# A two-block transformer step on one core: the chunked state-space part in another order

## The chip, the cores and the metric

The program runs as one launch on one core of a Trainium2 chip, in fp32 (matmuls on fp32 values split into two reduced parts). The metric is device time in microseconds, from the profiled execution and from timed runs. The engines: TensorE (PE in the rows; its weight loads PEld), VectorE (DVE), ScalarE (ACT), GpSimd (POOL), SyncE (SP), which issues most DMAs from one in-order queue.

## The reference, cut to what matters

272 tokens (16 meta tokens and 256 of x), width 1024. The first block has an attention half and a state-space half side by side, then a feed-forward part that picks single-neuron experts (PEER); the second block (two layers) follows and is not touched.

```
proj = rms_norm(h) @ w_in                       # q 512, k 128, v 128, u 512 columns
attn = sliding_window_attention(q, k, v)        # 8 heads, 2 key heads, sinks, 16 meta keys
# state-space half: 32 groups of 16 channels, each drives one 64-dim complex diagonal state
abar = exp((a_re + i a_im) * dt);  bbar = (abar - 1) / a * b
s_t  = abar * s_{t-1} + bbar @ u_t              # an associative scan over the 272 tokens
y    = Re(c @ s) + d * u
z    = gelu(y);  ssm = z * sigmoid(z @ glu_w + glu_b)
h    = h + concat(rms_norm(attn), rms_norm(ssm)) @ w_out
h    = h + peer_ffn(rms_norm(h))                # 8 heads x 16 experts of 16384
```

## The kernel before, in words

The state-space half is computed in 34 chunks of 8 tokens. `coefficients` makes the powers of abar (A), the discretized b (`bb`) and the maps `W` (8 taps by 16 channels into the 64 complex states of a group). `maps` transposes `W` on TensorE into `WT` and builds the rotation table `R` over the chunks. `enter` writes the projected rows u to DRAM and reads them back as `U`, chunk by chunk (the U bounce). `run` then multiplies U by WT (`st`, one input a chunk), rotates it by R, scans over the chunks (`sc`), rotates back (`S`), and forms y on TensorE from `T` (the response inside a chunk, a Toeplitz matrix) and from `G` (the outputs of the state). `outputs` builds `G` from c and A; `response` multiplies G by bd (bb spread out) into `K`, writes it to DRAM and reads it back 16 times shifted as `T`. After the Gelu, z goes to DRAM and comes back in another order as `zT`; the GLU matmuls follow, then the second half of the out-projection.

The big products lie in four scratch buffers t0 to t3 (`temp`), each handed from one tile to the next: a tile gets its buffer when all users of the tile before are done. PSUM banks are handed round in the same way, by tags: "p", "o", "y", "m" (transposes, scores, response) and "b" (state inputs, part of y, GLU).

`first_half` traces, in this order: the angles, the norm and its transposes (`turn`, whose `hH` ScalarE and `hL` VectorE write; the last `hL` is `c.split`), the u projection (four weight units of 128x1024, two of its eight row blocks each) with `coefficients` behind the first unit, then `enter`, `maps`, a 8 MB clearing of `wscr`, and then two strands that `Flow` interleaves: the state-space `run` in front, and as background `kv`, `q` and `attention` (with the first half of the out-projection, `out_part`). The numbers that both yield say how much of the background is traced between two steps of the front.

That tracing order is not the order of execution. A planner orders the instructions of each engine ahead of time: by its own cost model, it puts next what is ready, the one traced earliest first; something traced late that is ready early can go far ahead. `c.after(b, a)` (an order-only edge) keeps b behind a. The order of each engine and of SP's queue is then fixed in the program, and on the chip semaphores do the waiting.

Weights come through `Feed`: units of 512 KB are loaded by SP into five buffers, ScalarE rounds each to `H`, and GpSimd (P) or VectorE (V) subtracts to get `Lo`; `jobs` says which one per weight. Units 0 to 3 are wu, 4 and 5 wkv, 6 to 9 wq, 10 to 17 wo (10 to 13 for attention's half, 14 to 17 for the other), from 18 on wqy, the queries of PEER. A matmul of such values is three: H with H, and H with each Lo (lines 1678 to 1680).

Of the kernel before, what the change touches and what calls it, by code (L numbers as in the profile page):

```python
# [19 lines left out]
FT = mybir.dt.float32  # L20
# [4 lines left out]
OP = mybir.AluOpType  # L25
AX = mybir.AxisListType

T = 256
# [36 lines left out]
class Feed:  # L65


    def __init__(self, nc, wpool, spool, jobs, bufs, ahead):
        self.nc, self.wpool, self.spool, self.bufs, self.ahead = nc, wpool, spool, bufs, ahead
        self.units = []  # L70
        for ap, n, eng in jobs:
            for i in range(ap.shape[1]):
                self.units += [(ap[:, i, q * n:(q + 1) * n], n, eng[(2 * i + q) % len(eng)]) for q in range(2)]
        self.loaded = []
        self.cut = []
        self.taken = 0
        self.more = None
# [6 lines left out]
    def load(self, upto):  # L84
        while len(self.loaded) <= min(upto, len(self.units) - 1):
            ap, n, _ = self.units[len(self.loaded)]
            t = self.wpool.tile([128, 1024], FT, tag="w", name="w")[:, :n]
            self.nc.sync.dma_start(t, ap)
            self.loaded.append(t)
# [83 lines left out]
SJ = 8  # L173
# [3 lines left out]
def first_half(c):  # L177

    nc, tc, A = c.nc, c.tc, c.A
    V, G = nc.vector, nc.gpsimd  # L180
    f = Flow(c)
    with ExitStack() as ctx:
# [56 lines left out]
        for q in range(4):  # L239
            H, Lo = c.feed.take()  # L240
            for k2 in range(2):
                k = 2 * q + k2
                for ct in range(4):
                    s = slice(k2 * 512 + ct * 128, k2 * 512 + (ct + 1) * 128)
                    c.mm3(up[ct][:, :L], H[:, s], Lo[:, s], hH[:, k], hL[:, k], k == 0, k == 7)
                if k + 3 < 8:
                    turn(k + 3)
            if q == 0:
                ssm.coefficients()
        ssm.enter(up)  # L250
        ssm.maps()
        for i in range(4):
# [182 lines left out]
class Ssm:  # L435
# [9 lines left out]

    def product(self, re, im, a, b, t):

        V = self.V
        V.tensor_tensor(re, a[0], b[0], op=OP.mult)
        V.tensor_tensor(t[0], a[1], b[1], op=OP.mult)  # L450
        V.tensor_tensor(im, a[0], b[1], op=OP.mult)
        V.tensor_tensor(t[1], a[1], b[0], op=OP.mult)
        V.tensor_tensor(re, re, t[0], op=OP.subtract)
        V.tensor_tensor(im, im, t[1], op=OP.add)

# [27 lines left out]
    def coefficients(self):  # L483
# [28 lines left out]
        V.tensor_tensor(ci, t0, t1, op=OP.subtract)  # L512
        V.tensor_tensor(ci, ci, den, op=OP.mult)
        bre, bim = (P1(n).rearrange("p (j q) -> p j q", j=16) for n in ("bre", "bim"))
        bb = [one.tile([128, 16, 16], FT, name="bb%d" % i) for i in range(2)]
        shape = [128, 16, 16]
        cb = [t[:, :, None].to_broadcast(shape) for t in (cr, ci)]
        t = self.temp("tb", 2).rearrange("p (a j q) -> p a j q", j=16, q=16)
        self.product(bb[0], bb[1], (bre, bim), cb, [t[:, z] for z in range(2)])

        self.bd = [one.tile([128, 16, 2, 16], FT, name="bd%d" % i) for i in range(2)]
        for z in range(2):
            nc.gpsimd.memset(self.bd[z], 0.0)
            for g in range(2):
# [6 lines left out]
        t = [self.temp("tw", 2 + z) for z in range(2)]  # L531
        self.product(cut(self.W[0]), cut(self.W[1]), [A[:, z, :, :SJ, None].to_broadcast(shape) for z in range(2)],
                     [bb[z][:, :, None, :].to_broadcast(shape) for z in range(2)], [cut(x) for x in t])

    def enter(self, up):

        nc, c, one = self.nc, self.c, self.one
        uP = one.tile([128, 4 * L], FT, tag="uP", name="uP").rearrange("p (a j c) -> p a j c", a=4, j=SJ)
        self.U = U = one.tile([128, 32, SC], FT, name="U")
        for ct in range(4):  # L540
            nc.scalar.copy(uP[:, ct].rearrange("p j c -> p c j"), up[ct][:, :L].rearrange("p (c j) -> p c j", j=SJ))
            nc.sync.dma_start(c.udr[ct * 128:(ct + 1) * 128], uP[:, ct])
        src = c.udr.rearrange("(g q) j c -> q j g c", q=16)
        for j in range(SJ):
            m = SJ - 1 - j
            nc.sync.dma_start(U[16 * m:16 * m + 16], src[:, j])

    def maps(self):

        nc, c, V, P1, one = self.nc, self.c, self.V, self.P1, self.one  # L550
        self.WT = [one.tile([128, 16, 128], FT, tag="WT", name="WT", bufs=2) for z in range(2)]
        for z in range(2):
            for i in range(4):
                p = c.psum("m")
                for k in range(4):
                    nc.tensor.transpose(p[:, k * 128:(k + 1) * 128], self.W[z][:, (4 * i + k) * 128:(4 * i + k + 1) * 128], c.ident)
                nc.scalar.copy(self.WT[z][:, 4 * i:4 * i + 4].rearrange("p a b -> p (a b)"), p)

        self.R = R = one.tile([128, 2, 16, SC], FT, name="R")
        V.memset(R[:, 0, :, 0:1], 1.0)  # L560
        V.memset(R[:, 1, :, 0:1], 0.0)
        t = self.temp("tr", 2)[:, :512].rearrange("p (z j c) -> p z j c", z=2, j=16)
        for i in range(6):
            n = 2 ** i
            k = min(n, SC - n)
            self.product(R[:, 0, :, n:n + k], R[:, 1, :, n:n + k], [R[:, z, :, :k] for z in range(2)],
                         [self.cs[z][:, 1 + i, :, None].to_broadcast([128, 16, k]) for z in range(2)], [t[:, z, :, :k] for z in range(2)])
        self.mags = one.tile([128, 16, SC], FT, name="mags")
        nc.scalar.copy(self.mags, self.mag[:, 1, :, None].to_broadcast([128, 16, SC]))
        V.memset(self.mags[:, :, 0:1], 0.0)  # L570

    def outputs(self):

        nc, c, V, P1, one = self.nc, self.c, self.V, self.P1, self.one
        A = self.A
# [3 lines left out]
        a = [A[:, z, :, :, None].to_broadcast(shape) for z in range(2)]  # L579
        t = [self.temp("tg", 2 + z).rearrange("p (j m q) -> p j m q", j=16, q=16) for z in range(2)]  # L580
        V.tensor_tensor(self.G[0], C[0], a[0], op=OP.mult)
        V.tensor_tensor(t[0], C[1], a[1], op=OP.mult)
        V.tensor_tensor(self.G[0], self.G[0], t[0], op=OP.subtract)
        V.tensor_tensor(self.G[1], C[0], a[1], op=OP.mult)
        V.tensor_tensor(t[1], C[1], a[0], op=OP.mult)
        V.scalar_tensor_tensor(self.G[1], self.G[1], -1.0, t[1], op0=OP.mult, op1=OP.subtract)

    def response(self):
# [18 lines left out]
        nc.sync.dma_start(c.kdr.rearrange("(a p) n -> p a n", p=128), K.rearrange("p a m q -> p a (m q)"))  # L607
        self.T = [one.tile([128, 16, 128], FT, tag="WT", name="T", bufs=2) for z in range(2)]
        src = c.kdr.rearrange("(g q) n -> q g n", q=16)
        for h in range(2):  # L610
            for j in range(SJ):
                m = SJ - 1 - j
                nc.sync.dma_start(self.T[h][16 * m:16 * m + 16], src[:, 16 * h:16 * h + 16, 16 * m:16 * m + 128])

    def run(self, glu, out):
        nc, c, V, one = self.nc, self.c, self.V, self.one
        yield 8000

        st = self.temp("s", 0)[:, :2 * 16 * SC].rearrange("p (z j c) -> p z j c", z=2, j=16)
        for j0, n in ((0, 6), (6, 5), (11, 5)):  # L620
            for z in range(2):
# [5 lines left out]
                for g in range(2):  # L627
                    r = slice(64 * g, 64 * g + 64)
                    nc.scalar.copy(st[r, z, j0:j0 + n], v[r, :, g])
            yield 1500  # L630

        self.outputs()
        flat = lambda t: t.rearrange("p j c -> p (j c)")
# [6 lines left out]
        V.tensor_tensor(m1[:, 1], m1[:, 1], m2[:, 0], op=OP.subtract)  # L640
        yield 3000
        sc = room("sc", 3)
        for z in range(2):
            V.tensor_tensor_scan(flat(sc[:, z]), flat(self.mags), flat(m1[:, z]), 0.0, op0=OP.mult, op1=OP.add)
        yield 2000
        self.response()
        m1, m2 = room("m1", 0), room("m2", 1)
# [10 lines left out]
        yield 3000  # L658

# [4 lines left out]
        for ct in range(4):  # L664
            y = c.psum("yb"[ct % 2])
            for jj in range(4):
                j = 4 * ct + jj
                for g in range(2):
                    o = 2 * jj + g
                    m = nc.tensor.matmul(y[:, o * n:(o + 1) * n], self.T[j // 8][:, (2 * j + g) % 16], self.U[:, 2 * j + g, 2:],  # L670
                                         start=(o == 0), stop=False, skip_group_check=True)
# [9 lines left out]
            if ct % 2:  # L681
# [3 lines left out]
                for k in (ct - 1, ct):  # L685
                    nc.sync.dma_start(self.zT[:, k], c.zdr[k * 128:(k + 1) * 128].rearrange("p i c -> p (i c)"))
            yield 1500
        yield "exps"
        acc = [c.psum("b") for _ in range(2)]
        yield 8000  # L690
        for k in range(4):
            for co in range(4):
# [925 lines left out]
def body(tc, A, out):  # L1618
# [3 lines left out]
    with ExitStack() as ctx:  # L1622
# [23 lines left out]
        def evac(dst, src):  # L1646
# [3 lines left out]
            else:  # L1650
# [5 lines left out]
        LE = [P, P, V]  # L1656
        jobs = [(A["wu"], 1024, [P, P, V]), (A["wkv"], 1024, [P]), (A["wq"], 1024, [P]), (A["wo"][:, :2], 1024, [P, P, V]),
                (A["wo"][:, 2:], 1024, [P]), (A["wqy"], 1024, [P, V]),
                (A["ut"], 1024, [V]), (A["pv"], 1024, [V]), (A["we"], 1024, LE), (A["woe"], 1024, LE), (A["wod"][:, :2], 1024, LE),
# [213 lines left out]
```

## Time and profile before

| | before |
|---|---|
| median of 3 runs | 1415.31 us (1413.77 to 1418.36) |
| profiled execution | 1414.31 us, span 1412.3 us |
| TensorE busy | 1293.4 us (92%), mean granted clock 0.943 |
| VectorE busy | 935.5 us (66%) |
| ScalarE busy | 647.7 us (46%) |
| GpSimd busy | 457.5 us (32%) |
| HBM read, written | 233.24 MB, 28.90 MB |

Times inside the program are microseconds from the start of the span. "Busy" is the sum of the instructions' durations; neighbours on one engine overlap a little, so starts tell the pace better than durations. The granted clock of TensorE is a share of its full rate: 1.0 is 2.4 GHz, 0.5 is 1.2 GHz.

### The profile page before, as it was taken

The numbers are of one execution on the slowest core, as the hardware profiler recorded it, in microseconds if no ns is written. First come the engines' busy times: TensorE is split into PE (matmuls) and PEld (weight loads), VectorE is DVE, ScalarE is ACT, GpSimd is POOL, SyncE is SP. The second block draws the span as 40 slices with busy tenths as digits, with TensorE's granted clock in tenths as the row PEclk, the third lists the DMA queues.
The fourth block names the chain that finished last, engine by engine and source line by source line (L and its number), as shares of the span: only waits on it lengthen the run. The fifth ranks groups of instructions, "written<-read, shape, count | busy, mean of one in ns | idle before, by whom it ended". The sixth has DMA issues, their size and how long they took to land.

```text
span 1412.3 us, 21249 instructions
## 1 busy us (share of the span) xinstructions
PE 1293.4 (92%) x7800; PEld 1123.5 (80%) x7800; DVE 935.5 (66%) x2151; ACT 647.7 (46%) x1119; POOL 457.5 (32%) x237
## 2 busy tenths in 40 slices
PE   4566979899999999999899999999998989989998
PEld 3554868899999999999777888888876768765777
DVE  8845216889889766665578965555567775585834
ACT  4233315455455444444454444444454545433553
POOL 3140204257777878720000000000024226441243
PEclk9775769999999999999999999999999999997999
DMA  5653436478888777799799966566574335541331
GB/s 195 212 175 81 39 89 213 145 215 223 227 225 223 203 204 194 208 321 321 249 304 311 336 217 191 186 191 190 187 235 149 90 105 156 202 147 53 95 105 60
DMA packets 118520, 263.80 MB, mean 187 GB/s; under 512 B 36096, under 2 KB 50304, under 8 KB 117136
## 3 DMA queue, kind: packets, MB, share of 16 engines
q1 hardware_dynamic: 80336, 228.82, 51.6%
q0 software_dynamic: 20608, 8.46, 5.0%
q10 hardware_dynamic: 17472, 25.17, 5.0%
q8 instruction: 61, 1.00, 0.3%
q14 instruction: 43, 0.35, 0.1%
HBM read 233.24 MB, written 28.90 MB: 186 GB/s over the span
## 4 chain that ended last, share of the span: by engine, by line
PE 76%; DVE 16%; DMA 4%; issue 2%; ACT 2%; SPq 0%; DVEq 0%; ACTq 0%
PE ps L865 21%; PE ps L1678 9%; PE ps L1679 9%; PE ps L1680 9%; PE pr L1678 4%; PE pr L1680 4%; PE pr L1679 4%; DMA ga<-ascr 3%; PE m L1270 2%; PE ps L1078 2%; DVE Lo L102 2%; PE o L1315 1%; DVE rs L1695 1%; DVE rs L1696 1%; PE p L1678 1%
## 5 line engine op out<-in xcount | busy, mean ns | idle before, releaser
L101 ACT CAST H<-w 128x1024 fp32r<-128x1024 f32 (+1 forms) x370 | 386.5, 1046 | 495.0 <-PE ps L865 181.8
L102 DVE TENSOR_TENSOR Lo<-w,H 128x1024 fp32r<-128x1024 f32 x290 | 363.3, 1253 | 160.8 <-ACT H L101 160.4
L102 POOL TENSOR_TENSOR Lo<-w,H 128x1024 fp32r<-128x1024 f32 (+1 forms) x80 | 194.7, 2438 | 835.3 <-ACT H L101 815.3
L1678 PE MATMUL ps<-xH,H 128*128 128x256 f32 x1024 | 290.8, 284 | 0.0
L1679 PE MATMUL ps<-xL,H 128*128 128x256 f32 x1024 | 287.8, 281 | 0.0
L1680 PE MATMUL ps<-xH,Lo 128*128 128x256 f32 x1024 | 287.6, 281 | 0.0
L865 PE MATMUL ps<-H,a 128*128 128x512 f32 x1024 | 281.5, 397 | 4.1 <-ACT a L877 3.0
L1036 POOL DMA_INDIRECT wscr<-sent x128 | 239.6, 1872 | 87.8 <-issue 36.8
L865 PEld LDWEIGHTS ps<-H,a 128*128 128x128 f32 x1024 | 193.8, 189 | 50.3 <-ACT a L877 3.2
L1678 PEld LDWEIGHTS ps<-xH,H 128*128 128x128 f32 x1024 | 193.1, 189 | 0.0
L1679 PEld LDWEIGHTS ps<-xL,H 128*128 128x128 f32 x1024 | 193.1, 189 | 0.0
L1680 PEld LDWEIGHTS ps<-xH,Lo 128*128 128x128 f32 x1024 | 192.9, 188 | 0.0
L865 PE MATMUL ps<-Lo,a 128*128 128x512 f32 x512 | 161.8, 397 | 1.1 <-DVE Lo L102 1.0
L865 PEld LDWEIGHTS ps<-Lo,a 128*128 128x128 f32 x512 | 96.6, 189 | 25.2 <-DVE Lo L102 3.0
L875 DVE TENSOR_TENSOR act<-ga,act 128x256 f32<-128x256 f32 x128 | 47.4, 421 | 27.1 <-DMA ga<-ascr 26.8
L1678 PE MATMUL pr<-H,exH 128*128 128x512 f32 x128 | 54.3, 426 | 0.9 <-ACT exH L1118 0.9
L1678 PE MATMUL pr<-H,oxH 128*128 128x512 f32 (+1 forms) x128 | 52.7, 414 | 1.1 <-ACT oxH L1118 1.1
L878 DVE TENSOR_TENSOR a<-act,a 128x256 fp32r<-128x256 f32 x128 | 53.5, 419 | 0.0
L877 ACT CAST a<-act 128x256 fp32r<-128x256 f32 x128 | 51.5, 402 | 2.8 <-DVE act L875 2.8
L1680 PE MATMUL pr<-H,exL 128*128 128x512 f32 x128 | 52.7, 412 | 0.0
L1680 PE MATMUL pr<-H,oxL 128*128 128x512 f32 (+1 forms) x128 | 52.6, 411 | 0.0
L1679 PE MATMUL pr<-Lo,exH 128*128 128x512 f32 x128 | 52.4, 410 | 0.0
(486 smaller groups left out, 2001.8 us busy)
## 6 DMA issues: line engine op xcount, KB each, us to landing
w<-in_ut SPq DMA_DIRECT2D x128, 512.0 KB
w<-in_pv SPq DMA_DIRECT2D x128, 512.0 KB
ascr<-ga ACTq DMA_DIRECT2D x64, 256.0 KB
ga<-ascr SPq DMA_DIRECT2D x64, 256.0 KB
w<-in_we SPq DMA_DIRECT2D x32, 512.0 KB
w<-in_wod SPq DMA_DIRECT2D x28, 512.0 KB
wscr<-zero ACTq DMA_DIRECT2D x4, 2048.0 KB
w<-in_wqy SPq DMA_DIRECT2D x16, 512.0 KB
```

Source lines behind the costliest of these rows:

```text
L101: self.last = self.nc.scalar.copy(H, self.loaded[u])
L102: eng.tensor_sub(Lo, self.loaded[u], H.bitcast(FT))
L865: nc.tensor.matmul(acc[2 * th + n], a[:, s], b[:, n * 512:(n + 1) * 512], start=first and e == 0, stop=last and e == 2)
L875: V.tensor_tensor(src, ga[:, blk % 2], src, op=OP.mult)
L877: copied = nc.scalar.copy(aH, src)
L878: V.tensor_sub(aL, src, aH.bitcast(FT))
L1036: ins = c.nc.gpsimd.indirect_dma_start(out=c.wscr.rearrange("i b (t o) -> (i b t) o", o=1), out_offset=bass.IndirectOffsetOnAxis(ap=t.bitc ...
L1078: nc.tensor.matmul(p[:, a * 128:(a + 1) * 128], o1[:, a], o2[:, a], start=True, stop=True)
L1270: nc.tensor.matmul(sp[:, :off + nk], q(h)[:, ts], k(h)[:, :off + nk], start=True, stop=True)
L1678: nc.tensor.matmul(o, ah, bh, start=first, stop=False)
L1679: nc.tensor.matmul(o, ah, bl, start=False, stop=False)
L1680: nc.tensor.matmul(o, al, bh, start=False, stop=last)
```

## The change

1. `coefficients` is cut in two: the products `bb` and `W` (with `bd`) move to a new `powers`, traced after the u projection, and the four multiplies of `bb` are kept behind the last row split `c.split` on VectorE.
2. `maps` keeps only the transposes of `W`; it is traced inside `run`, after kv and the first step of q. `WT` now lies in t2 and t3.
3. The table `R` moves into a new `tables`, and its 36 products go from VectorE to GpSimd. Its scratch and `bb` lie in one new tile `pre`, in the buffer that `T` gets later.
4. `outputs` (G) is traced right after `tables`, before kv. Three of its multiplies are kept behind the last instruction of `W`. Its scratch lies in t0 and t1, which `W` holds until its transposes are done.
5. `response` is traced after the state inputs and ahead of the scan (before: behind the scan). `T` is one tile, read back by 8 DMAs of 256 KB (before: 16 of 128 KB).
6. Loads of weight units are kept behind the bounces in SP's queue: unit 10 behind the last read of U, 11 to 14 behind the last of T, 15 to 18 behind the last of zT.
7. `Lo` of wu is made by GpSimd alone (before: one of three by VectorE); of wkv, wq, wo and wqy by VectorE alone (before: GpSimd for wkv, wq and half of wo, shared for the rest).
8. The yields in `run` change (1500 to 500 and 3000 to 2000 at places, 3000 added behind `maps`).

```diff
@@ first_half
+        ssm.powers()
         ssm.enter(up)
-        ssm.maps()
+        ssm.tables()
+        ssm.outputs()
@@ Ssm.product
-    def product(self, re, im, a, b, t):
+    def product(self, re, im, a, b, t, E=None, behind=None):
+        E = E or self.V
+        ops = [E.tensor_tensor(re, a[0], b[0], op=OP.mult), E.tensor_tensor(t[0], a[1], b[1], op=OP.mult),
+               E.tensor_tensor(im, a[0], b[1], op=OP.mult), E.tensor_tensor(t[1], a[1], b[0], op=OP.mult)]
+        for op in ops if behind is not None else ():
+            self.c.after(op, behind)
+        E.tensor_tensor(re, re, t[0], op=OP.subtract)
+        return E.tensor_tensor(im, im, t[1], op=OP.add)
@@ Ssm.powers (cut from coefficients)
+    def powers(self):
+        self.pre = one.tile([128, 4096], FT, tag="T", name="pre")
+        bb = [self.pre[:, 256 * z:256 * z + 256].rearrange("p (j q) -> p j q", j=16) for z in range(2)]
-        self.product(bb[0], bb[1], (bre, bim), cb, [t[:, z] for z in range(2)])
+        self.product(bb[0], bb[1], (bre, bim), cb, [t[:, z] for z in range(2)], behind=c.split)
...
-        self.product(cut(self.W[0]), cut(self.W[1]), [A[:, z, :, :SJ, None].to_broadcast(shape) for z in range(2)],
+        self.wdone = self.product(cut(self.W[0]), cut(self.W[1]), [A[:, z, :, :SJ, None].to_broadcast(shape) for z in range(2)],
@@ Ssm.enter: the last read of U is kept
-            nc.sync.dma_start(U[16 * m:16 * m + 16], src[:, j])
+            self.had = [nc.sync.dma_start(U[16 * m:16 * m + 16], src[:, j])]
@@ Ssm.maps, Ssm.tables
-        self.WT = [one.tile([128, 16, 128], FT, tag="WT", name="WT", bufs=2) for z in range(2)]
+        self.WT = [self.temp("WT", 2 + z)[:, :2048].rearrange("p (j n) -> p j n", j=16) for z in range(2)]
...
+    def tables(self):
+        G = nc.gpsimd
-        t = self.temp("tr", 2)[:, :512].rearrange("p (z j c) -> p z j c", z=2, j=16)
+        t = self.pre[:, 512:1024].rearrange("p (z j c) -> p z j c", z=2, j=16)
...
-                         [self.cs[z][:, 1 + i, :, None].to_broadcast([128, 16, k]) for z in range(2)], [t[:, z, :, :k] for z in range(2)])
+                         [self.cs[z][:, 1 + i, :, None].to_broadcast([128, 16, k]) for z in range(2)], [t[:, z, :, :k] for z in range(2)], E=G)
@@ Ssm.outputs
-        t = [self.temp("tg", 2 + z).rearrange("p (j m q) -> p j m q", j=16, q=16) for z in range(2)]
-        V.tensor_tensor(self.G[0], C[0], a[0], op=OP.mult)
-        V.tensor_tensor(t[0], C[1], a[1], op=OP.mult)
+        t = [self.temp("tg", z).rearrange("p (j m q) -> p j m q", j=16, q=16) for z in range(2)]
+        for op in (V.tensor_tensor(self.G[0], C[0], a[0], op=OP.mult), V.tensor_tensor(t[0], C[1], a[1], op=OP.mult)):
+            c.after(op, self.wdone)
...
-        V.tensor_tensor(self.G[1], C[0], a[1], op=OP.mult)
+        c.after(V.tensor_tensor(self.G[1], C[0], a[1], op=OP.mult), self.wdone)
@@ Ssm.response
-        self.T = [one.tile([128, 16, 128], FT, tag="WT", name="T", bufs=2) for z in range(2)]
-        for h in range(2):
-            for j in range(SJ):
-                m = SJ - 1 - j
-                nc.sync.dma_start(self.T[h][16 * m:16 * m + 16], src[:, 16 * h:16 * h + 16, 16 * m:16 * m + 128])
+        self.T = one.tile([128, 4096], FT, tag="T", name="T").rearrange("p (g n) -> p g n", g=32)
+        for m in range(SJ):
+            t = nc.sync.dma_start(self.T[16 * m:16 * m + 16], src[:, :, 16 * m:16 * m + 128])
+        self.had.append(t)
@@ Ssm.run
         yield 8000
+        self.maps()
+        yield 3000
...
-            yield 1500
-
-        self.outputs()
+            yield 500
+        self.response()
...
-        self.response()
@@ Ssm.run, behind the reads of zT and ahead of the GLU
+        for u, i in [(10, 0)] + [(u, 1) for u in range(11, 15)] + [(u, 2) for u in range(15, 19)]:
+            if u < len(c.feed.issued):
+                c.after(c.feed.issued[u], self.had[i])
@@ body
-        jobs = [(A["wu"], 1024, [P, P, V]), (A["wkv"], 1024, [P]), (A["wq"], 1024, [P]), (A["wo"][:, :2], 1024, [P, P, V]),
-                (A["wo"][:, 2:], 1024, [P]), (A["wqy"], 1024, [P, V]),
+        jobs = [(A["wu"], 1024, [P]), (A["wkv"], 1024, [V]), (A["wq"], 1024, [V]), (A["wo"], 1024, [V]), (A["wqy"], 1024, [V]),
```

## Rows read from the trace of the kernel before

**Rows 1.** Stretches: us, busy of each engine, granted clock, DMA share, GB/s.
```profile
0.00:226.00 226.00, 151.79 (x820) 127.69 (x821) 121.79 (x285) 72.28 (x152) 50.29 (x27) 0.78 0.49 130
226.00:1412.30 1186.30, 1141.59 (x6981) 995.77 (x6981) 813.73 (x1867) 575.47 (x969) 407.23 (x210) 0.97 0.65 198
```

**Rows 2.** TensorE's timeline: start, duration, line, tiles, count [idle before <- releaser].
```profile
47.83 0.28 PE L228 MATMUL m<-cstt,mt 16*128 16x16 f32 x1 [14.97 <-DVE hL L233]
...
54.38 0.29 PE L1680 MATMUL o<-hH,Lo 128*128 128x272 f32 x1
...
78.91 0.76 PE L1678 MATMUL p<-H,hH 128*128 128x512 f32 x1 [12.25 <-DVE ks L288]
...
97.36 0.39 PE L1679 MATMUL p<-Lo,hH 128*128 128x512 f32 x1
97.59 0.39 PE L1680 MATMUL p<-H,hL 128*128 128x512 f32 x1
...
115.55 1.94 PE L330 MATMUL m<-cstt,xs 128*128 128x128 f32 x8 [14.77 <-DVE xs L323]
...
126.59 3.66 PE L599 MATMUL m<-G,bd 128*32 128x128 f32 x64
...
151.16 0.50 PE L1678 MATMUL p<-H,aH 128*128 128x512 f32 x1 [0.68 <-ACT aH L421]
...
164.86 0.53 PE L670 MATMUL y<-U,T 128*128 128x32 f32 x4
...
187.47 1.09 PE L677 MATMUL b<-S,G 128*128 128x64 f32 x4
...
201.75 1.69 PE L693 MATMUL b<-zT,glu 128*128 128x256 f32 x6 [3.83 <-DMA zT<-zdr]
...
207.75 0.50 PE L1678 MATMUL p<-H,zH 128*128 128x512 f32 x1 [0.60 <-ACT zH L720]
...
225.87 0.39 PE L1678 MATMUL ps<-hH,H 128*128 128x256 f32 x1
```

**Rows 3.** VectorE's timeline, 0 to 114 us.
```profile
10.03 2.33 DVE L1696 SCALAR_TENSOR_TENSOR rs<-rs 128x3 f32<-128x3 f32 x1
...
17.43 2.54 DVE L581 TENSOR_TENSOR G<-pk,A 128x2304 f32<-128x2304 f32 x1
...
28.35 0.50 DVE L233 SCALAR_TENSOR_TENSOR hL<-m,pka,hH 128x272 fp32r<-128x272 f32 x1
...
34.07 2.28 DVE L449 TENSOR_TENSOR W<-A,bb 128x2048 f32<-128x2048 f32 x1
...
70.67 0.88 DVE L284 TENSOR_REDUCE kss<-ks 128x2 f32<-128x128 f32 x3 [3.73 <-ACT ks L283]
...
72.00 2.27 DVE L1689 TENSOR_SCALAR ri<-rs 128x6 int32<-128x6 int32 x1
...
97.22 1.29 DVE L637 TENSOR_TENSOR m<-s,R 128x1088 f32<-128x1088 f32 x1 [3.72 <-ACT s L629]
...
106.78 1.21 DVE L102 TENSOR_TENSOR Lo<-w,H 128x1024 fp32r<-128x1024 f32 x1
...
113.15 0.69 DVE L657 TENSOR_TENSOR S<-m,m 64x512 f32<-64x512 f32 x1
```

**Rows 4.** GpSimd by line and shape: count, busy us, mean ns, idle before.
```profile
L1357 POOL TENSOR_TENSOR emx<-emx,vz 128x512 f32<-128x512 f32 x2 | 2.6, 1298 | 1.3 <-DVE vz L1203 1.3
...
L1444 POOL TENSOR_TENSOR kn<-ovz 128x128 f32<-128x128 f32 x2 | 0.8, 400 | 2.4 <-ACT ovz L1191 2.4
```

**Rows 5.** GpSimd's timeline, 0 to 60 us.
```profile
9.97 4.72 POOL L102 TENSOR_TENSOR Lo<-w,H 128x1024 fp32r<-128x1024 f32 x2 [7.99 <-ACT H L101]
27.34 3.35 POOL L102 TENSOR_TENSOR Lo<-w,H 128x1024 fp32r<-128x1024 f32 x1 [12.65 <-ACT H L101]
```

**Rows 6.** SP's queue, 0 to 200 us: start, time of all issues, count.
```profile
61.95 11.19 SPq L546 DMA_DIRECT2D U<-udr  x8
...
134.05 12.30 SPq L613 DMA_DIRECT2D T<-kdr  x16
```

More of the change, by code (lines that the diff above doesn't have):

```diff
@@ L74, in __init__ @@
         self.loaded = []
+        self.issued = []
         self.cut = []
@@ L87, in load @@
             t = self.wpool.tile([128, 1024], FT, tag="w", name="w")[:, :n]
-            self.nc.sync.dma_start(t, ap)
+            self.issued.append(self.nc.sync.dma_start(t, ap))
             self.loaded.append(t)
@@ L444, in temp @@
         return self.one.tile([128, 2304], FT, tag="t%d" % i, name=name)
-    def product(self, re, im, a, b, t):
[L448 to L454, printed above, removed]
+    def product(self, re, im, a, b, t, E=None, behind=None):
[6 more added lines that the diff above has]
+        return E.tensor_tensor(im, im, t[1], op=OP.add)
     def angles(self):
@@ L513, in coefficients @@
         V.tensor_tensor(ci, ci, den, op=OP.mult)
+        self.c12 = cr, ci
+    def powers(self):
+        nc, c, V, P1, one, A = self.nc, self.c, self.V, self.P1, self.one, self.A
+        cr, ci = self.c12
         bre, bim = (P1(n).rearrange("p (j q) -> p j q", j=16) for n in ("bre", "bim"))
-        bb = [one.tile([128, 16, 16], FT, name="bb%d" % i) for i in range(2)]
+        self.pre = one.tile([128, 4096], FT, tag="T", name="pre")
+        bb = [self.pre[:, 256 * z:256 * z + 256].rearrange("p (j q) -> p j q", j=16) for z in range(2)]
         shape = [128, 16, 16]
@@ L557, in maps @@
                 nc.scalar.copy(self.WT[z][:, 4 * i:4 * i + 4].rearrange("p a b -> p (a b)"), p)
+    def tables(self):
+        nc, c, V, one = self.nc, self.c, self.V, self.one
+        G = nc.gpsimd
         self.R = R = one.tile([128, 2, 16, SC], FT, name="R")
@@ L640, in run @@
         V.tensor_tensor(m1[:, 1], m1[:, 1], m2[:, 0], op=OP.subtract)
-        yield 3000
+        yield 2000
         sc = room("sc", 3)
@@ L657, in run @@
                 V.tensor_tensor(S[z][r, :, g], m1[r, z, :, 1:SC - 1], m2[r, 1 - z, :, 1:SC - 1], op=(OP.subtract, OP.add)[z])
-        yield 3000
+        yield 2000
         zc = self.temp("zc", 3)[:, :32 * (SC - 2)].rearrange("p (g c) -> p g c", g=32)
@@ L669, in run @@
                     o = 2 * jj + g
-                    m = nc.tensor.matmul(y[:, o * n:(o + 1) * n], self.T[j // 8][:, (2 * j + g) % 16], self.U[:, 2 * j + g, 2:],
+                    m = nc.tensor.matmul(y[:, o * n:(o + 1) * n], self.T[:, 2 * j + g], self.U[:, 2 * j + g, 2:],
                                          start=(o == 0), stop=False, skip_group_check=True)
@@ L685, in run @@
                 for k in (ct - 1, ct):
-                    nc.sync.dma_start(self.zT[:, k], c.zdr[k * 128:(k + 1) * 128].rearrange("p i c -> p (i c)"))
+                    t = nc.sync.dma_start(self.zT[:, k], c.zdr[k * 128:(k + 1) * 128].rearrange("p i c -> p (i c)"))
             yield 1500
+        self.had.append(t)
         yield "exps"
```

## The prediction, made before the change was run

> **What bounds the kernel now.** I read the stretches of the span first. From 226 us to the end TensorE is busy 1141.6 of 1186.3 us at a granted clock of 0.97; ahead of 226 us it is busy 151.8 of 226.0 us at 0.78 [rows 1]. The edited code lies almost wholly in that first block. Behind it the work is a queue of matmuls with next to no idle time, so an earlier end of the block moves everything behind it, and the end of the program, by as much. The step at which the block ends is the first matmul of the query projection, at 225.87 [rows 2].
>
> Then TensorE's timeline of the block. Four waits stand out in its brackets: 14.97 us for a split `hL` (VectorE) at 47.83, 12.25 us for `ks` at 78.91, 14.77 us for `xs` at 115.55, and 3.83 us for `zT` coming back from DRAM at 201.75 [rows 2]. VectorE's timeline names what held the first: at 34.07 the first of six 2.28 us instructions of `W` goes ahead of the split; and a `G` product at 17.43 (2.54 us) goes ahead of the very first split [rows 3]. So instructions that nobody needs yet are placed wherever VectorE has a gap, ahead of short ones on the path. Last, the end of the block is serial: out-projection of attention from 151.16 to 164.9, y from 164.86 to 188.6, DRAM bounce to 201.75, GLU, then the other out-projection from 207.75 [rows 2].
>
> **The change part by part.** I follow one marker at a time on TensorE, "before" by rows 2.
>
> *End of the u projection.* The `bb` product, and `W` with it, is queued behind the last split, `G` behind `W`. That takes away the 15.0 us wait, and some 2.1 us by which `G` held the first split (free at 19.9; its input was there near 17.8). Sum 17.1: the last of these matmuls ends at 37.5 instead of 54.6 (54.38 and its 0.29, less overlap).
>
> *Table R to GpSimd.* 36 products, 3168 elements a partition in all. No row shows one on GpSimd; its rows give 0.40 us at 128 elements and 1.30 at 512 [rows 4], so 2.34 ns an element and 0.1 us each: 11.0 us together, an estimate. Cover: GpSimd has nothing to do between its early Lo's [rows 5]. Its inputs are there at 8 us, so I place it between 8 and 30 us, where VectorE's work on the path is the x norm and splits. The row to weigh is at 10.03: a three-element instruction of the norm took 2.33 us beside a GpSimd Lo, whereas the split at 28.35 took 0.50 during another [rows 3, 5]; the split reads PSUM. So two SBUF instructions exclude each other. Ends 0 and +11.0; I take 1.5 on the norm, and count it against the warm-up that the earlier first split may save, so 0.
> The Trainium skill says so more sharply ("SBUF — State Buffer", section "SBUF: two separate sides"): VectorE and GpSimd share one port pair, the one that begins holds it for the whole instruction and the other blocks. The trace agrees (2.33 us against the 4.72 us of two Lo's). It speaks against this part: by it R saves VectorE nothing wherever both have work. Its outcome is the second rival.
>
> *VectorE up to the query projection.* `q` needs PSUM banks that kv's tail frees, and that tail is traced behind `W` and `G`; now these sit in its way. The last split: three more follow the one at 28.35, each behind a group of matmuls of some 2 us, less the 2.1 above, so about 33.0. From there (all by rows 3, with the 0.07 by which neighbours overlap taken off): `bb`, an eighth of `W` in elements, about 2.0; `W` 6 x 2.20 = 13.2; two Lo of wkv, now on VectorE, 2 x 1.2 = 2.4 (as at 106.78); `G` 6 x 2.47 = 14.8; two Lo of wq 2.4; kv's tail from 70.67 to 78.9 less two blocks behind GpSimd Lo's, that at 72.00 and one as long behind it, 8.2 - 4.2 = 4.0. End near 72.0: `q` starts there instead of 78.91. So 10 of the 17 us are given back. `G`'s scratch now uses `W`'s buffers, so its second half waits on VectorE for TensorE's transposes of `W`; TensorE did kv and those transposes in 12 us (54.6 to 66.7, where the wait begins), so is free for them by about 48, so I cost that at 0. Without that cover it is up to 5 us, with kv's tail queued behind it.
>
> *State inputs and response.* The U bounce ended 18.5 us after its u projection (54.6 to 73.1 [rows 6]); it now ends near 56, and no weight load lies ahead of it. So the state matmuls run in the wait for `q`, and `q` needs only 48 x 0.23 = 11.2 (97.36 to 97.59), plus the response's 3.6 (126.59): end 86.8 instead of 100.8.
>
> *q's tail.* Before, its reductions and norm shared VectorE with the scan, 16.7 us from 100.8 to the scores at 117.5. The scan's chain (97.22 to 113.8, 16.6 us [rows 3]) now begins near 72 and is over at 88.6. Left are squares and reductions 2.5, norm 2.6, the two `xs` 1.3, transposes 1.9, a Lo: 9.4. Scores at 96.2, 21.3 us earlier.
>
> *T and y.* `T` is now 8 transfers of 256 KB, before 16 of 128 KB; these took 12.3 us of SP's queue [rows 6]. Response at 83 to 87, then write and read back in 12 to 18 us: T near 104. Before it was asked for at 134 to 146, beside the attention, and y stood behind the whole out-projection. Now y can run inside the attention. It took 23.7 us, with 1.09 us for a group at the end and 0.53 for one at the start: about 13 at full clock. Ends 0 (all in idle slots) and 23.7; I take 13, the nearer to a TensorE that does not rest.
>
> *End of the block.* Attention from scores to the end of its out-projection took 47.4; less the response's 3.6, plus y's 13, gives 56.8: end 153.0 instead of 164.9. `zT` needs 13.2 us after y (188.6 to 201.75), and y ends before the out-projection's 13.7, by 139.3, so it is there at 152.5 or earlier: the bounce is covered. GLU's 32 matmuls cost 32 x 0.28 = 9.0 (1.69 for six at 201.75), then 1.7 to the first out-projection matmul: 163.7 instead of 207.75. The last stretch (18.1 us) loses some 2 us, since the norm of z no longer waits for GpSimd Lo's: 179.8 instead of 225.9. Gain 46.1.
>
> *Weight loads.* SP's queue is in order. Unit 10 now stands behind the U reads, 11 to 14 behind T, 15 to 18 behind `zT`; behind a late one every further load waits, and so do the ACT cast, VectorE's Lo and TensorE. With T at 104 and attention's out-projection at 139, and unit 14 there for the first 2.8 us of the last one, I cost it at 0. If T or `zT` came late it is 5 to 8 us. All Lo of wo and wqy on VectorE: 16 more x 1.2 there, against blocks of 2 us that go; TensorE is idle only 4 in 100 behind 226 us [rows 1]. 0, ends -4 and +4.
>
> The sum is made against the profiled run, 1414.31 us (span 1412.3 and 2 around it): 1368.2. The median of the runs, 1415.31, is 1.0 above it, which I leave in the range.
>
> **The rivals.**
> *y stays behind attention's out-projection* (1387.4). The order on TensorE is fixed ahead of time; before, y came behind although T's last issue at 146.4 [rows 6] was 18 us ahead of y. If the plan again expects T late, only the 21.3 and 3.6 us of an earlier attention and the 2 at the end are left: 26.9 gained. For it: that distance of 18 us. Against: T is asked for some 45 us earlier.
> *R's lock lands on W and G* (1379). If GpSimd takes R up while VectorE works through `bb`, `W` and `G`, the 11.0 us lie on the path to `q`. For it: 72.00, where a six-element shift took 2.27 us beside a Lo. Against: R's inputs are ready at 8 us. (This is what the skill's rule makes of it.)
> *VectorE becomes the bound of the block, and the result is slower* (1425). VectorE alone serves `W`, `G`, scan, both tails and 14 Lo that were GpSimd's. If kv's tail is queued behind the scan as well (11.5 net) with R's lock (11.0) and four more Lo (4.8), `q` starts at 99, 20 us later than before; S and T are then too late for y to move, and the pinned loads starve the last out-projection by up to 8 us. What the response and q's tail give (3.6 + 14) doesn't pay for it: about +11. It decides from a `q` start at about 95. Against: kv's tail is traced ahead of the scan.
> *No change to be told* needs two of these at once with half their prices.
>
> **How the numbers follow.** Forecast 0.60, own range 1350 to 1382 (y from 0 to 23.7 us, GLU, weights); y behind 0.19; R's lock 0.11; slower 0.07; within 0.3% 0.03. A change under about 0.3% (4 us) can't be told from none. The range 1345 to 1400 holds the first three. Faster 0.90, same 0.03, slower 0.07.
>
> **What would show it.** The 15.0 us wait of TensorE for `hL` gone, last u matmul near 37; `q` started by 68 to 76, with a wait of over 20 us named to `ks` ahead of it; y's matmuls ahead of the end of attention's out-projection; no wait for `zT`, or one under 3 us; R's products on GpSimd done by about 30; the first query-projection matmul near 180. A `q` start past 85, or y's matmuls behind the out-projection, would make the number wrong; a block end beyond 220 the sign.

## The result and the profile after

| | time, us | against before | clock | block end |
|---|---|---|---|---|
| before | 1415.82 median of 4 | | 0.943 | 225.87 |
| changed | 1384.39 (1384.07 to 1385.08, 4 runs) | 0.9778 [0.9761, 0.9795] | 0.953 | 200.34 |
| predicted | 1368 | | | 179.8 |

The change is faster by 31.4 us. The sign held, and the time lies in the range of 1345 to 1400, though just outside the forecast's own 1350 to 1382; the forecast gain was 46 to 47, half as much again as came. The profiled execution took 1384.22 us, its span 1382.4. "Block end" is again the first matmul of the query projection. Windows ahead of and behind it, to set beside [rows 1]:

```profile
0.00:200.34 200.34, 150.85 (x819) 126.86 (x819) 117.64 (x263) 72.05 (x151) 26.22 (x49) 0.81 0.56 149
200.34:1382.40 1182.06, 1139.99 (x6981) 994.10 (x6981) 813.89 (x1873) 574.90 (x969) 393.70 (x204) 0.98 0.64 198
```

Between the two profiled executions 25.5 us were gained in the block, 4.4 behind it. TensorE's timeline of the block, for [rows 2]:

```profile
21.03 0.28 PE L229 MATMUL m<-cstt,mt 16*128 16x16 f32 x1 [4.80 <-DVE hL L234]
...
37.98 0.29 PE L1698 MATMUL o<-hH,Lo 128*128 128x272 f32 x1
...
65.98 0.45 PE L639 MATMUL b<-U,WT 128*128 128x68 f32 x1 [3.88 <-DMA U<-udr]
...
75.79 0.77 PE L1696 MATMUL p<-H,hH 128*128 128x512 f32 x1
...
93.00 0.40 PE L1698 MATMUL p<-H,hL 128*128 128x512 f32 x1
...
104.71 1.94 PE L333 MATMUL m<-cstt,xs 128*128 128x128 f32 x8 [11.31 <-DVE xs L326]
106.58 0.85 PE L369 MATMUL m<-kT,qT 64*128 64x144 f32 x2
...
138.56 0.50 PE L1696 MATMUL p<-H,aH 128*128 128x512 f32 x1 [0.68 <-ACT aH L424]
...
143.47 0.53 PE L684 MATMUL y<-U,T 128*128 128x32 f32 x4
...
150.75 1.09 PE L691 MATMUL b<-S,G 128*128 128x64 f32 x4
...
165.25 0.77 PE L1696 MATMUL p<-H,aH 128*128 128x512 f32 x1
...
176.05 0.59 PE L712 MATMUL b<-zT,glu 128*128 128x256 f32 x2
...
184.02 0.50 PE L1696 MATMUL p<-H,zH 128*128 128x512 f32 x1 [0.90 <-ACT zH L739]
...
200.34 0.39 PE L1696 MATMUL ps<-hH,H 128*128 128x256 f32 x1 [1.00 <-DVE hL L764]
```

The wait of 14.97 us for `hL` and that for `zT` are gone. Two things are not as forecast. The state matmuls stand ahead of `q`, but wait for `U` until 65.98; so the sign of a long wait for `ks` ahead of `q` is not there. And y runs not inside the attention but behind the first 12 matmuls of its out-projection, and takes 21.8 us there (143.47 to 165.25).

What held `U`: the chain of waits goes, between 39 and 66 us,

```profile
39.65 18.49 DMA wscr<-zero
58.16 7.69 DMA U<-udr
```

and ScalarE's and SP's timelines show the same from the issuing side:

```profile
39.65 12.87 ACTq L256 DMA_DIRECT2D wscr<-zero  x2
52.62 1.04 ACT L102 CAST H<-w 128x1024 fp32r<-128x1024 f32 x1 [12.21 <-issue]
```
```profile
48.23 10.91 SPq L556 DMA_DIRECT2D U<-udr  x8
...
96.67 9.69 SPq L625 DMA_DIRECT2D T<-kdr  x8
```

The clearing of `wscr`, four transfers of 2 MB that the program issues on ScalarE, now lies ahead of the U bounce; issuing the last two holds ScalarE for 12.87 us, and with it the casts and copies behind. The Trainium skill ("DMA: Bandwidth & Descriptors", section "Issuing engines are not separate DMA queues") says that transfers begun by different engines run on the same DMA engines and interleave, and calls the time to issue one usually small beside the transfer itself. The chain agrees with the first; with the second it does not, since 12.87 us of issuing stand beside the 18.49 us of the clear in the chain.

### The profile page after: what moved, and what is told of

It reads as the page before. It is cut to its first block, busy times and chain, and to the rows that moved or that the text cites. A ratio compares the mean times of both kernels' runs of the same rounds, so it can differ in the third digit from the quotient of the medians.

```text
span 1382.4 us, 21238 instructions
## 1 busy us (share of the span) xinstructions
PE 1290.8 (93%) x7800; PEld 1121.0 (81%) x7800; DVE 931.5 (67%) x2135; ACT 646.9 (47%) x1119; POOL 419.9 (30%) x253
## 4 chain that ended last, share of the span: by engine, by line
PE 77%; DVE 13%; DMA 6%; ACT 2%; issue 2%; SPq 0%; ACTq 0%; DVEq 0%
PE ps L884 20%; PE ps L1696 10%; PE ps L1697 10%; PE ps L1698 10%; PE pr L1696 4%; PE pr L1698 4%; PE pr L1697 4%; DMA ga<-ascr 3%; PE m L1289 2%; DVE Lo L103 2%; PE ps L1097 2%; PE o L1334 1%; DMA wscr<-zero 1%; DVE act L894 1%; PE m L369 1%
## 5 line engine op out<-in xcount | busy, mean ns | idle before, releaser
L103 DVE TENSOR_TENSOR Lo<-w,H 128x1024 fp32r<-128x1024 f32 x310 | 387.5, 1251 | 183.3 <-ACT H L102 179.8
L103 POOL TENSOR_TENSOR Lo<-w,H 128x1024 fp32r<-128x1024 f32 (+1 forms) x60 | 142.1, 2373 | 629.1 <-ACT H L102 604.2
```

Source lines behind the costliest of these rows:

```text
L103: eng.tensor_sub(Lo, self.loaded[u], H.bitcast(FT))
```

## The experiments

All times are ratios to the kernel before, run on the same chip beside it; the changed kernel has 0.978. No kernel here leaves anything out. First the parts of the change, each alone or undone.

**The pins on VectorE alone.** Kernel before, with two edits:

```
-  self.product(bb[0], ...)          (traced in coefficients)
+  self.product(bb[0], ..., behind=c.split)   (in powers)
+  for op in (three multiplies of G): c.after(op, self.wdone)
```

> Kernel before with one part of the change alone: bb is queued behind the last split, G behind W; R, Lo's, state order, T and weight loads stay as before. Main theory: the 15.0 us wait for hL goes, the u projection ends near 38 instead of 54.6, kv's tail is then behind W and G, q starts about 10 earlier than 78.9 less what W and G give back, y stays behind attention's out-projection: time 1400 to 1405 (-11 to -15 against before, 1415.8). Rival (VectorE gives it all back before q): the u projection ends near 38 all the same, but q starts at 76 to 80 and the time is 1411 to 1416.

Measured 1414.95 us, 1.001 [0.9996, 1.0025]: the rival, with `q` at 80.66 just past its 76 to 80. The u projection ends at 36.2, 18 us earlier, and all of it is given back before `q`. Rows of TensorE, VectorE and GpSimd:

```profile
80.66 0.77 PE L1685 MATMUL p<-H,hH 128*128 128x512 f32 x1 [20.36 <-DVE ks L289]
```
```profile
69.97 4.69 DVE L593 SCALAR_TENSOR_TENSOR G<-G,tg 128x2304 f32<-128x2304 f32 x1
74.58 2.55 DVE L590 TENSOR_TENSOR G<-G,tg 128x2304 f32<-128x2304 f32 x1
```
```profile
60.74 11.50 POOL L102 TENSOR_TENSOR Lo<-w,H 128x1024 fp32r<-128x1024 f32 x3 [24.09 <-ACT H L101]
```

VectorE reaches kv's tail only behind `W`, R (some 8 us, placed among G's instructions) and G, and a G instruction takes 4.69 us while GpSimd's three Lo's run, 2.55 behind them. This is the lock of the prediction's second rival, on the Lo's rather than on R. The pins gain only with the other parts.

**R back on VectorE.** Changed kernel, `E=G` of the 36 products left out.

> Changed kernel with R's 36 products back on VectorE. In the run with the pins alone they took VectorE about 9 us between W and G. Theory 1 (VectorE's chain up to kv's tail sets q's start, and R on GpSimd takes its 9 us off it): q starts 6 to 9 us later than 75.8, ratio 0.983 to 0.985. Theory 2 (U's reads behind the clear set the state matmuls and those set q, so VectorE has 3 us and more to spare, and the first split comes 1 to 2 us earlier without GpSimd beside it): ratio 0.976 to 0.980.

Measured 1383.94, 0.9797 [0.9768, 0.9826]: theory 2; R's place decides nothing that can be told. Here the plan puts R between the row splits (17.0 to 29.6), where VectorE waits for ScalarE anyway, and `ks` is ready at 70.4. The first split comes without GpSimd beside it (wait of 0.15 us at 19.11, against 4.80 at 21.03), so `q` starts 3.3 us earlier, at 72.53; the attention, at a mean clock of 0.59 against 0.63, gives most of it back, and the block ends at 200.07. So R on GpSimd costs the first split about 2 us, which do not reach the block's end.

**Without the pins of the weight loads.** The loop of `c.after(c.feed.issued[u], self.had[i])` is left out.

> Changed kernel without the pins of the weight loads 10 to 18 behind U, T and zT. Main theory: the loads run ahead of the T transfers on SP's queue, T comes later, and y goes wholly behind attention's out-projection with its zT bounce of some 13 us bare: 1393 to 1400 (+9 to +15 against 1384.4), a zT wait of TensorE of over 5 us back. Rival (pins do nothing that counts, my prediction's 0 for them): 1383 to 1387, y's place decided by the order of response and T alone.

Measured 1396.13, 0.9872 [0.9836, 0.9909]: the main theory. TensorE's timeline:

```profile
156.15 0.53 PE L684 MATMUL y<-U,T 128*128 128x32 f32 x4
...
183.83 0.76 PE L712 MATMUL b<-zT,glu 128*128 128x256 f32 x1 [3.88 <-DMA zT<-zdr]
...
192.54 0.70 PE L712 MATMUL b<-zT,glu 128*128 128x256 f32 x2 [3.25 <-DMA zT<-zdr]
```

All 48 matmuls of the out-projection run first, then y, then the bare bounce. The reason expected was wrong: T's reads are issued at 99.06 to 108.7, only 2.4 us later than in the changed kernel and 47 us ahead of y. So on the chip T does not decide y's place. That the pins act in the plan (with units 11 to 14 ordered behind T, the planner finds y ready in the gap behind unit 10's 12 matmuls) is how I read it, not shown. Of the 13.1 us by which the block ends later (213.48), 3.6 are there before y: the scores start at 110.17 instead of 106.58.

**The response at its old place, behind the scan.**

```
-        self.response()      (ahead of the scan)
+        self.response()      (behind the second tensor_tensor_scan)
```

> Changed kernel with the response (16 small matmuls, K, T's write and read back) at its old place behind the scan. Theory 1 (my prediction's step: an early T is what lets y leave its place behind the out-projection): T is asked for some 15 us later, y waits for it or goes behind, zT is bare, ratio 0.983 to 0.990. Theory 2 (the pins of the weight loads alone opened y's place; T has 30 us to spare between its landing near 108 and y at 143.5): y begins at 141 to 144 as in the changed kernel, q ends some 2 us earlier, ratio 0.976 to 0.980.

Measured 1388.43, 0.981 [0.9783, 0.9837]. T's reads are issued 23 us later, from 119.95, and y still begins at 144.48: theory 2 on y's place, though the ratio lies between the ranges of both. The block ends 1.2 us later than in the changed kernel; whether the time differs can't be told, the intervals overlap. So the early response isn't what let y move.

**Lo of wqy shared with GpSimd as before.** One word in `jobs`, `[V]` to `[P, V]`.

> Changed kernel with the Lo's of wqy shared between GpSimd and VectorE as before. Theory 1 (behind the block the change gained 4.4 us since no long GpSimd Lo holds VectorE's split xL in the query projection): the wait for xL there is back at about 5 us instead of 0.8, time +3 to +5 us, ratio 0.980 to 0.982. Theory 2 (the 4.4 us are the weight loads' other order): wait for xL as in the changed kernel or without effect, ratio 0.977 to 0.979.

Measured 1390.09, 0.9828 [0.98, 0.9856]; the wait of the query projection's second half is back (before 4.97, changed 0.84):

```profile
234.51 0.69 PE L762 MATMUL ps<-cstt,act 128*128 128x128 f32 x2 [4.96 <-DVE xL L764]
```

By its size this wait is nearly all of the gain behind the block (4.1 of 4.4), but with it back the stretch behind the block grew by only 2.4 us, from 1182.06 to 1184.47; so theory 1 holds for the wait, and for a little over half of the time. Here the block also ended 3.8 us later (204.13); its cause wasn't followed.

Next, the U bounce behind the clear of `wscr`.

**The clear early.** Its four transfers pinned behind the casts of the u projection:

```
-            c.after(z, c.turned)
+            c.after(z, c.turns[(0, 2, 4, 6)[i]])
```

> Changed kernel with one edit: the four transfers that clear the 8 MB of wscr on ScalarE's queue are pinned behind the row block's casts 0, 2, 4 and 6 (about 10 to 25 us) and no longer behind the last cast, just ahead of the U bounce. Main theory (the clear goes ahead of the U bounce in the DMA engines, and ScalarE stands 12.9 us issuing it): U reads land near 56 instead of 65.8, no ScalarE issue of over 5 us, q ends near 85 to 87 instead of 93.3, scores near 97 instead of 106.6, time -8 to -10 us against the changed kernel (1384.4), that is 1374.5 to 1376.5. Rival (kv's tail on VectorE ends at 73.1 and holds q, whatever U does): the block gains at most the 3 us between 73.1 and q's start at 75.8, 1381 to 1384. Second rival (the clear only moves its collision to the weight loads of the u projection): u projection ends later than 38.1, no gain or a loss up to 5 us.

Measured 1394.03, 0.9855 [0.9817, 0.9893], slower than the changed kernel, which no theory had. SP's U reads are all issued by 53.8 instead of 59.1 and no issue holds ScalarE, but the plan moved along: the state matmuls went behind `q`'s first 24, and uP's copies, behind `bd`'s as in the changed kernel, start at 40.86 instead of 38.19, since `bb` is ready later. `q` starts at 74.44, and ends at 97.7.

**The order pinned again.** State matmuls ahead of `q`, uP's copies ahead of bd's, a Lo behind W's third product:

```
+                for m in c.qs: c.after(m, ssm.stm)
+        for b in self.bdc: c.after(b, u)
+                c.after(c.feed.subs[5], ssm.wops[2])
```

> The early clear of wscr once more (pinned behind casts 0, 2, 4, 6), with the three places pinned at which the order written for the engines had moved along with it: q's matmuls behind the last state matmul, the copies of bd behind those of uP, the second Lo of wkv behind W's third product. Theory A (U's reads behind the clear were what held the state matmuls; then the end of kv's tail on VectorE, 73 to 74, holds q, with the state matmuls done before it): state matmuls done by 70, q starts at 73 to 75 and, without 20 state matmuls in it, ends at 86 to 90 instead of 93.3; block end 4 to 6 us earlier than 200.3, time 0.974 to 0.976 of before (changed kernel: 0.978). Theory B (the clear costs nothing, since VectorE sets both q and the scan): q ends at 92 to 94, ratio 0.977 to 0.979.

Measured 1390.71, 0.9835 [0.9799, 0.9871], and again not the order wanted: the state matmuls came behind k's transposes, which stood for `ks` (18.66 us, to 73.26). `q` ended at 105.1. It tells theory A from B no more than the first.

**k's transposes behind the state matmuls too.** `c.qs` now holds them and the mean tokens' matmul as well.

> The early clear, with all that TensorE does for k's transposes and the mean tokens also pinned behind the last state matmul (in the run before, the state matmuls had been put behind them and TensorE stood 18.7 us for ks). Theory A (U's reads behind the clear held the state matmuls; now VectorE's ks at 73 to 74 sets q): state matmuls done by 66 to 70, q starts at 73 to 75, ends at 86 to 90 (changed kernel 93.3), scores by 98 to 102 (106.6), ratio 0.973 to 0.976. Theory B (the clear costs nothing): q ends at 92 to 94, ratio 0.977 to 0.979. If even with q ended by 90 the time stays at 0.978 or above, what is gained at q is lost again between the scores and the out-projection.

Measured 1375.25, 0.9717 [0.9689, 0.9746]: theory A by `q` and the scores (the state matmuls end at 73, not by 70), and 0.6% better than the changed kernel. TensorE's timeline:

```profile
57.70 0.88 PE L648 MATMUL b<-U,WT 128*128 128x68 f32 x3 [3.10 <-DMA U<-udr]
...
72.77 0.80 PE L1705 MATMUL p<-H,hH 128*128 128x512 f32 x1
...
89.12 0.40 PE L1707 MATMUL p<-H,hL 128*128 128x512 f32 x1
...
96.62 0.61 PE L373 MATMUL m<-kT,qT 64*128 64x144 f32 x1
...
192.78 0.38 PE L1705 MATMUL ps<-hH,H 128*128 128x256 f32 x1 [1.00 <-DVE hL L773]
```

U is there 8.3 us earlier (19.6 us behind the u projection instead of 27.7), all state matmuls run ahead of `q`, and the scores start at 96.62, where the prediction had put them (96.2). Of these 10.0 us the block keeps 7.6; 2.5 go in the attention (34.5 us from scores to out-projection at a mean clock of 0.59, against 32.0 at 0.65). The 10.0 us belong to the early clear and the pins together: the pins with the clear at its old place were not run.

**kv's tail ahead of four of G's instructions**, on top of that:

```
+            for op in ssm.late: c.after(op, kn)
```

> The kernel of the run before (early clear, state matmuls ahead of q) with one more edit: four of G's six instructions are put behind kv's tail on VectorE. Theory A (kv's tail, not the state matmuls, then holds q): ks comes at 62 to 66 instead of 73, q starts at 66 to 69 where the state matmuls end, ends at 80 to 84; 5 to 7 us earlier than without the edit, ratio 0.968 to 0.972. Rival (G's 10 us only move behind ks and hold the scan and with it q's reductions): q ends earlier, but the scores start at most 2 us earlier than without the edit.

Measured 1382.71, 0.977 [0.974, 0.9801]. `ks` is ready at 63, as expected, yet `q` starts at 79.90, 7 us later. ScalarE's row, first of the run before, then of this one:

```profile
63.46 1.34 ACT L653 COPY s<-b 64x204 f32<-64x204 f32 x4 [8.24 <-DVE G L606]
```
```profile
70.64 1.34 ACT L655 COPY s<-b 64x204 f32<-64x204 f32 x4 [15.50 <-DVE G L608]
```

The copies of the state inputs wait for G: `s` lies in t0, which holds G's scratch since the change, and the state matmuls wait for these copies to free their banks. A G put later holds both. Neither theory had it. With a buffer of its own for `s` it wasn't tried.

Last, y. Windows of the changed kernel (the clock is the third number from the end): y at the start, the rest of y, the out-projection behind it, and its end.

```profile
143.47:150.00 6.53, 6.53 (x58) 6.53 (x56) 0.67 (x1) 1.10 (x2) 0.00 (x0) 0.95 0.01 3
150.00:165.25 15.25, 15.25 (x73) 15.25 (x73) 2.36 (x2) 2.65 (x4) 0.00 (x0) 0.50 0.15 17
165.25:170.00 4.75, 4.75 (x14) 3.73 (x13) 0.52 (x1) 0.38 (x1) 0.00 (x0) 0.52 0.46 86
170.00:176.05 6.05, 6.05 (x26) 4.58 (x25) 2.71 (x4) 1.05 (x1) 0.00 (x0) 1.00 0.54 112
```

Over y's first groups of eight matmuls, 0.89 us each, the clock stands near 2.4 GHz, then it is at 1.2 GHz, 1.71 us each, and so is the out-projection's first part behind. By the profile, which models the ends of matmuls, TensorE was busy for all of 15.25 us, with matmuls and with weight loads. It was so in the kernel before, where y stood alone behind the out-projection; its first 5.2 us and the rest:

```profile
164.80:170.00 5.20, 5.20 (x44) 5.16 (x43) 1.09 (x3) 2.71 (x3) 3.32 (x2) 0.90 0.00 0
170.00:188.50 18.50, 18.50 (x87) 18.38 (x87) 0.00 (x0) 0.77 (x2) 0.00 (x0) 0.50 0.12 15
```

The Trainium skill ("TensorE: Matmul & The Clock Gate", section "HAM oscillation — how this bites in real kernels") ties such a fall to waits between bursts of matmuls; here the profile shows no wait inside y (15.25 of 15.25 us busy), and the clock fell all the same.

**y woven into the out-projection**, two of its matmuls between y's groups, the first group behind its 13th (`c.outs[12]`):

```
+                for j, m in enumerate(ssm.ys):
+                    c.after(m, c.outs[12 + 2 * j])
```

> Changed kernel with y's 16 groups of matmuls spread over attention's out-projection: the first behind its 12th matmul as now, then two of its 1-bank-wide matmuls between neighbouring groups. Work is the same, only its order differs. Theory 1 (the granted clock falls because y's small matmuls stand in one piece, and stays low for the rest of the out-projection): the stretch from y's first matmul to the end of the out-projection, 143.5 to 176.2 = 32.7 us, shrinks to 22 to 26, time 1374 to 1378. Theory 2 (y's cost is its own, in fixed time for each small matmul, wherever it stands): the stretch stays 31 to 34, time 1383 to 1386. Theory 3 (the weave delays zT, whose bounce is then bare): stretch shorter, but a wait for zT of 5 us or more ahead of GLU, 1384 to 1390.

Measured 1390.38, 0.9835 [0.9796, 0.9874]. Windows of y's stretch, of what follows up to the other out-projection, and of its start:

```profile
155.00:168.00 13.00, 13.00 (x98) 12.22 (x98) 1.69 (x2) 1.55 (x4) 0.00 (x0) 1.00 0.17 20
168.00:185.61 17.61, 10.25 (x37) 7.68 (x37) 5.09 (x8) 3.75 (x7) 0.00 (x0) 0.90 0.67 205
185.61:195.00 9.39, 9.39 (x31) 8.04 (x32) 3.84 (x11) 3.17 (x6) 0.00 (x0) 0.53 0.25 94
```

Theory 1, and a loss behind it as in theory 3. The clock stays at 2.4 GHz, and y with the rest of the out-projection takes 22.6 us (146.60 to 169.15) instead of 32.7. But TensorE is idle for 7.4 of the next 17.6 us: 3.5 around GLU, whose `zT` is bare, and then

```profile
185.61 0.50 PE L1702 MATMUL p<-H,zH 128*128 128x512 f32 x1 [3.92 <-ACT zH L745]
```

ahead of the other out-projection, which starts at the lower clock. The chain of waits leads from this `zH` over the Lo and the cast of a wo unit to that unit's load, 177.30 to 182.08: the loads pinned behind `zT` came late with it. The prediction had priced that (5 to 8 us if `zT` came late). The weave without these pins wasn't run. The block ends 6.3 us later.

**The same earlier and closer:** from the third matmul on, one between groups.

```
+                    for m in y: c.after(m, c.outs[2 + j])
+                    c.after(c.outs[3 + j], y[-1])
```

> Changed kernel with y's 16 groups woven into attention's out-projection as in the first weave, but from its third matmul on and with one of its matmuls between neighbouring groups, so that y ends some 9 us earlier. Theory 1 (the large matmuls between them hold the clock): y from 140 to 158, out-projection ends at 164 to 168 instead of 176.2, zT bare for 4 to 6 us, block end at 190 to 195 instead of 200.3, ratio 0.970 to 0.974. Theory 2 (one large matmul between the groups is too little, the clock falls all the same): y ends at 164 to 168, out-projection at 174 to 177, ratio 0.977 to 0.980. Theory 3 (as in the first weave, the wait for zT costs the clock in GLU and the other out-projection as well): out-projection ends by 168, block end not before 198.

Measured 1390.23 (1382.68 to 1399.15), 0.9808 [0.9761, 0.9855]. In the profiled execution, the slowest, the clock was already low when y began, and stayed so, as theory 2 has it; the other three have higher mean clocks (0.946 to 0.951 against 0.939) and no trace:

```profile
144.20:160.00 15.80, 15.80 (x69) 15.13 (x69) 3.76 (x9) 4.02 (x5) 0.00 (x0) 0.50 0.00 1
```

**y between the steps of the attention.**

```
+                    for m in y: c.after(m, c.stages[j][-1])
+                    for m in c.stages[j + 1]: c.after(m, y[-1])
```

> Changed kernel with y's 16 groups put between the 16 steps (transposes, products with v) of the attention, where TensorE waits for ScalarE's copies, instead of in one piece inside the out-projection. Theory 1 (my prediction's step: T is there at about 108, so y can run inside the attention, costs 13 us or less there, and zT's bounce is covered by the out-projection): the steps of the attention end at 146 to 152 instead of 137, the out-projection runs at the higher clock and ends at 160 to 167 instead of 176.2, no zT wait, block end at 184 to 191 instead of 200.3, ratio 0.965 to 0.971. Theory 2 (y's groups at the lower clock cost their 1.7 us wherever they stand and the idle slots are too short): steps end at 158 to 162, out-projection at 172 to 176, ratio 0.976 to 0.978. Theory 3 (Gelu and the copies of y hold ScalarE, on which the attention's steps wait): slower than the changed kernel, above 0.980.

Measured 0.9755 [0.9685, 0.9825], from two of its four executions; the four lay between 1369.51 and 1398.83, so it can't be ranked with the changed kernel. The trace is of one at 1391.3: y there runs at the lower clock throughout, each group 1.6 to 1.7 us, and the steps end at 169 instead of 137:

```profile
124.16:150.00 25.84, 25.84 (x113) 23.77 (x113) 3.51 (x5) 9.93 (x25) 0.00 (x0) 0.50 0.19 58
```

That is theory 2 at a higher price. The one execution at 1369.51 is near what the prediction asked for, and has the highest mean clock of the four (0.961 against 0.939 to 0.945); without its trace the clock as its cause is argued, not shown.

## Why the prediction was partly right

- *End of the u projection*: 37.5 predicted, 37.98 plus 0.29 measured. The 15.0 us came as named. The other 2.1 did not come where I had put them and are luck: the first splits came no earlier (second batch of matmuls at 21.03, before 20.43), for now GpSimd's products stood beside VectorE's; but without the 15 us wait the last matmuls ran at the higher clock, 0.13 us apart instead of 0.23.
- *Table R*: its products ran on GpSimd from 7.09 to 25.6, some 15.0 us of them and not 11.0. They cost the first split about 2 us, which I had set off to 0; at the block's end nothing of it can be told. The rival of R's lock on `W` and G did not come.
- *VectorE up to q*: kv's tail was done at 73.1, predicted 72.0. Right. But `q` started at 75.8: state matmuls, not `ks`, stood before it.
- *State inputs* is the step that failed first: "it now ends near 56". My 18.5 us for the U bounce ran only to the end of SP's issues, not to the landing, and I looked at SP's queue alone. The clear ran beside the bounce before, too (issued on ScalarE's queue between 48.78 and 65.0), but there nobody waited for U. Now the clear went ahead of it and U's landing was waited for: the bounce took 27.7 us, and U was there at 66. The scan, which should have run from 72, ran from 89.07 to 102.4, so *q's tail* failed with it: scores at 106.6 instead of 96.2. With the clear out of the way and the order held, 10.0 of these 10.4 us came back. That they then met the forecast is partly luck, since `q` ended at 89.5 and not 86.8, and the tail behind it was shorter.
- *T and y*: T was asked for from 96.7, early enough. y did leave its place, though through the load pins, which I had costed at 0, and not by an early T; without them the time is the first rival's case (1396, priced at 1387). The size failed: 21.8 us and not 13. The two rows behind the 13 are of unlike matmuls (1.09 us for four of 64 columns, 0.53 for four of 32); like for like a group of eight took 0.89 us at 2.4 GHz, 14.2 for the sixteen. And the clock fell inside y, as it had in the kernel before. Some 4 more were lost around it (69.5 us from the scores to GLU, predicted 56.8): 2.0 in the attention, 2.0 in the out-projection. The first weave shows that the stretch has those 10 us in it at 2.4 GHz.
- *End of the block*: `zT` covered, GLU to the other out-projection 8.0 us, predicted 10.7; my row for GLU's price lay in a stretch at a clock of 0.68. The last stretch 16.3, predicted 16.1. 10.4 + 12.7 - 2.7 + 0.2 make the missing 20.5, to rounding.
- *Behind the block*: 4.4 gained, just past the ends of 4 that I gave for Lo's on VectorE. Up to 4.1 of it is the wait for `xL`; undone alone, 2.4 came back.

That the time lies in the range is partly luck, too: the two terms that failed cost 23 us together, and what made up for 7 of them was a GLU priced too high and the gain behind the block, which I had put at 0.

The fastest version by its median is the changed kernel with the early clear and the order pinned: 1375.25 us.

## What to carry to other kernels

Who moves a transfer forward should list what every queue has under way at its new time: the same DMA engines serve them all (here the bounce took 27.7 us beside the clear and 19.6 with the clear issued earlier). Where a planner writes the order, an edit moves more than it names (the first two runs with the early clear came out slower than the changed kernel, each with instructions moved that no edit named), so read the new order before believing a price, and look at which scratch the moved instructions share. A price for small matmuls taken at the high clock needs a reason why the clock will hold there, and rows of like matmuls.

## What the runs showed that I had not expected

Issuing two 2 MB transfers in a row held ScalarE for 12.87 us; spread over some 20 us, in the runs with the early clear, none held it over 1.95 us. TensorE's clock fell to 1.2 GHz inside y with the engine busy throughout, and stayed at 2.4 GHz with two matmuls of 512 columns between y's groups. With one, starting at the lower clock, it did not rise; whether the start or the mixture decides is open. GpSimd's small products took 0.24 to 0.32 us at 16 and 32 elements a partition, the very first 1.03.
